# A two-layer hybrid backbone on one core: the order in which the input projections are written, with the first branch's queries behind its keys and the last gate chunk, the last recurrent chunk and the values moved behind the queries

## The chip, the core and the metric

The kernel runs on one core of one Trainium2 chip. The metric is the device time of one execution in microseconds (us); three executions of the kernel before gave 3127.03, 3131.85 and 3134.9 us, and their median, 3131.85 us, is the number to compare with.

The engines are named as the profile names them: PE is TensorE (matmuls), PEld its weight loads, DVE is VectorE, ACT is ScalarE, POOL is GpSimd, and SP is SyncE, whose queue issues every DMA of this kernel. Each engine works through its own instructions in order.

## The reference

The kernel computes two layers of a diffusion backbone on a latent stream of 1024 tokens and a context of 256 tokens, 1024 channels wide. The part of a layer around the change is this:

```
h = modulate(rms_norm(x, g_pre_mix), sh1, sc1);  z = h @ w_in
qa, ka, va, qb, kb, vb, xr, gr = split_columns(z)
qa, ka = apply_axial_rope(rms_norm(qa)), apply_axial_rope(rms_norm(ka))
out_a = global_block_attention(qa, [ka_c, ka], [va_c, va])          # branch a
qb, kb = apply_axial_rope(qb), apply_axial_rope(kb)
out_b = window_sink_attention(qb, kb, vb, kb_c, vb_c, sink)         # branch b
xr = centred_dwconv(xr, conv_w, conv_b)
h_f = directional_rglru(xr, ...)                                    # recurrence, forwards
h_b = directional_rglru(flip(xr), ...)                              # and backwards
out_c = (h_f + flip(h_b)) * gelu(gr)                                # branch c
x = x + gt1 * rms_norm([out_a, out_b, out_c] @ w_out, g_post_mix)
x = x + gt2 * rms_norm(sq_relu_mlp(modulate(rms_norm(x)), w1, w2), g_post_mlp)
```

The first layer also carries the context stream on to its end; the second layer needs it only for keys, values and the recurrence.

## The kernel before

Channels lie on the 128 partitions, tokens along the free axis, in three token tiles: 0 and 1 are the halves of the latent stream (512 tokens each) and 2 is the context (256). Every dense product is made of three matmuls on operands that were split into a high and a low part (`dense`, L497 to L499), over eight blocks of 128 input channels: 24 matmuls for a chunk of 128 output channels and one token tile. The code splits each weight in two: ACT copies it to `whi` (L134) and POOL or DVE makes `wlo` (L475).

**The projections.** The chunks of `w_in` have names: `x0` to `x3` feed the recurrence, `g0` to `g3` its gates (the gelu branch `gr`), `kF` and `kL` are the keys of the first and of the later attention branch, `F0`, `F1` and `L0`, `L1` their queries, and `v` the values of both. In both layers the first branch is b (window attention with a sink) and the later one a. `OPT[l]["ORD"]` writes out the order for layer l: `"g3:201"` is chunk `g3` for the token tiles 2, 0 and 1, `"F0:20"` the first queries for tiles 2 and 0. In layer 1 tile 2 is left out of everything but keys and x. A token `"F;L0:20,L1:20"` weaves two streams: the stacks of branch F (`kstacks`, L836: the keys are read back from DRAM and split into `kh` and `kl`) and the projections after the semicolon. A token `"L"` makes the stacks of the later branch. The results of a query or key chunk go through `qk_evac` (norm for branch a, rotation, DMA to DRAM), those of x through `xr_evac` (the convolution), those of g through `gr_evac`.

**What runs beside them.** Four generators are woven by rates: `conv_all` and `lru_all` for the recurrence, `side`, which walks through `ORD` and then the output projections, and `heads`, which makes the attention. The recurrence goes chunk by chunk, c0 to c3. Chunk c needs `x<c>` and `g<c>`. Its gates are 36 small matmuls (`gate`, L681 to L683), then come ACT's tanh, then exp and ln, and DVE's products and scans (L689, L708, L717, L720, L725); the result `hs` is written to DRAM (L733). tanh and gelu lie in one table set of ACT, exp and ln in another, and the helper `act` loads the other set wherever the order of writing changes from one kind to the other (L130).

`heads` waits until the last value tile exists, and `attend_prep` until all stacks of the branch do. It reads a query tile back (`qf`), splits it on ACT (`qh`), lets PE make scores from the high parts alone (`mx`, L885, L897, L905) and DVE reduce them to row maxima, which PE spreads (`pm`, L918). `attend_units` makes the full scores (`sc`, L954), ACT the exponentials (`prob`), and PE the products with the values (`pv`, L973) and the denominators (`den`, L1004). `out_lru` begins the output projection (`yps`) when all four recurrent chunks are done.

The gates decide one more thing: a recurrent chunk that is begun before the first attention job is prepared makes the gates of both directions at once; one that is begun later makes them one direction after the other, with a longer pause.

A scheduler then places the instructions of each engine in an order near that of writing. The function that names the order of weights from the same table is `entries`.

```
run(chain(*[step(t) for t in cf["ORD"][:cf["NX"]]]))            # the first two tokens of ORD
...
def side():
    for t in cf["ORD"][cf["NX"]:]:
        yield from step(t)
...
def heads():
    yield from wait(lambda: (1, 3) in V)
    yield from attention(jobs, (len(jobs) - 1,))
```

Of the kernel before, what the change touches and what calls it, by code (L numbers as in the profile page):

```python
# [32 lines left out]
    {"SPLIT": ((0,), (2, 1)), "JC": 16, "J": 16, "PRE": 4, "NP": 0, "RB": 1, "OL": (4, 1), "LEAD": 4,  # L33
     "MERGE": 1, "CAHEAD": 2, "NX": 2, "RO": 1.0, "RC": 2.0, "MR": 0.55, "TT0": (0, 2), "ADD_POOL": 4,
     "MUL_POOL": 0,
# [5 lines left out]
     "MUL_POOL": 0,  # L41
# [3 lines left out]
)  # L45
# [1318 lines left out]
```

## Time and profile before

| | |
|---|---|
| median of three executions | 3131.85 us |
| the profiled execution | 3129.46 us |
| its span, first to last instruction | 3127.4 us |
| PE busy | 2922.9 us, 93% |
| PEld, DVE, ACT, POOL busy | 71%, 55%, 40%, 38% |
| mean granted TensorE clock | 0.966 |

The profiled execution is 2.4 us under the median and 2.1 us over its own span. A share of busy time is a mean over stages that have different limits. The granted clock has two levels in this trace, 1.0 (2.4 GHz) and 0.5 (1.2 GHz), so a mean of 0.80 over a stretch says that 40% of it went by at the lower one. The name behind an arrow (`<-`) is what ended the idle time just before an instruction. A wait that is named counts only on the engine that bounds its stage.

### The profile page before, as it was taken

What the parts mean: (1) busy time and instruction counts of PE and PEld (TensorE: products, weight loads), DVE (VectorE), ACT (ScalarE), POOL (GpSimd) and SP (SyncE); (2) the same over time, 40 slices, a digit from 0 to 9 for tenths busy, and PEclk for the clock granted to TensorE, in tenths of its full rate; (3) what the DMA queues carried; (4) which work ended last, traced back from release to release, by engine and by line L of the source; (5) the groups of instructions that cost most, each with busy time, mean ns of one, the idle gap of its engine ahead of it and who ended that gap; (6) DMA issues with size and microseconds to landing.
All of it is one profiled execution on the core that took longest, in us unless ns stands there. A gap on an engine that the chain in (4) does not pass through costs nothing. (4 is left out here: it accounts for less than half of the span.)

```text
span 3127.4 us, 39445 instructions
## 1 busy us (share of the span) xinstructions
PE 2922.9 (93%) x14562; PEld 2227.4 (71%) x14562; DVE 1712.6 (55%) x2714; ACT 1255.1 (40%) x2347; POOL 1189.5 (38%) x919
## 2 busy tenths in 40 slices
PE   6998889998999999999899899689998999999997
PEld 4877544546867888888888688554456888888886
DVE  6765575554476133234884576776454562333465
ACT  4677243355243312213543368733354332122222
POOL 1453343344454222322533333353354553333232
PEclk9999799999999999999999999889998999999999
DMA  7343321123355222111643322330024241111241
GB/s 246 114 149 117 131 85 43 48 66 121 123 174 181 75 65 81 39 39 65 195 134 106 117 65 80 103 110 31 14 86 149 81 139 51 44 44 51 75 145 54
DMA packets 176338, 299.86 MB, mean 96 GB/s; under 512 B 24593, under 2 KB 38417, under 8 KB 176145
## 3 DMA queue, kind: packets, MB, share of 16 engines
q1 hardware_dynamic: 176144, 297.35, 28.9%
q8 instruction: 114, 1.87, 0.2%
q14 instruction: 80, 0.65, 0.1%
HBM read 262.14 MB, written 35.13 MB: 95 GB/s over the span
## 5 line engine op out<-in xcount | busy, mean ns | idle before, releaser
L475 POOL TENSOR_TENSOR wlo<-raw,whi 128x512 fp32r<-128x512 f32 x484 | 687.7, 1437 | 957.7 <-ACT whi L134 319.5
L1191 DVE TENSOR_TENSOR acc<-acc,m 128x512 f32<-128x512 f32 (+1 forms) x488 | 322.3, 676 | 318.7 <-PE m L1184 316.8
L1183 PE MATMUL m<-h1lo,whi 128*128 128x512 f32 (+1 forms) x1296 | 476.6, 369 | 7.3 <-DVE h1lo L1173 7.3
L1184 PE MATMUL m<-h1hi,wlo 128*128 128x512 f32 (+1 forms) x1296 | 474.3, 368 | 0.0
L1182 PE MATMUL m<-h1hi,whi 128*128 128x512 f32 (+1 forms) x1296 | 459.4, 370 | 7.2 <-DVE accc L1191 4.8
L134 ACT ACTIVATE whi<-raw 128x512 fp32r<-128x512 f32 x600 | 352.7, 621 | 149.5 <-DMA raw<-in_w 72.2
L497 PE MATMUL m<-hhi,whi 128*128 128x512 f32 x1024 | 403.3, 395 | 5.3 <-ACT hhi L134 5.3
L498 PE MATMUL m<-hlo,whi 128*128 128x512 f32 x1024 | 399.9, 391 | 2.8 <-DVE hlo L513 2.8
L499 PE MATMUL m<-hhi,wlo 128*128 128x512 f32 x1024 | 399.8, 391 | 0.0
L1173 DVE TENSOR_TENSOR h1lo<-relu,h1hi 128x512 fp32r<-128x512 f32 (+1 forms) x160 | 130.5, 816 | 446.8 <-ACT h1hi L134 446.6
L134 ACT ACTIVATE relu<-m 128x512 f32<-128x512 f32 (+1 forms) x160 | 88.5, 553 | 692.8 <-PE m L499 679.9
L1169 POOL TENSOR_TENSOR relu<-relu 128x512 f32<-128x512 f32 (+1 forms) x160 | 161.8, 1011 | 422.1 <-ACT relu L134 398.9
L1183 PEld LDWEIGHTS m<-h1lo,whi 128*128 128x128 f32 x1296 | 246.8, 191 | 50.2 <-DVE h1lo L1173 9.3
L1182 PEld LDWEIGHTS m<-h1hi,whi 128*128 128x128 f32 x1296 | 244.2, 190 | 53.0 <-DVE accc L1191 6.7
L1184 PEld LDWEIGHTS m<-h1hi,wlo 128*128 128x128 f32 x1296 | 246.6, 190 | 41.0
L497 PEld LDWEIGHTS m<-hhi,whi 128*128 128x128 f32 x1024 | 193.4, 189 | 47.1 <-ACT hhi L134 6.9
L979 POOL TENSOR_TENSOR prob<-prob 128x1024 f32<-128x1024 f32 (+2 forms) x62 | 137.3, 2215 | 229.8 <-ACT prob L134 128.7
L498 PEld LDWEIGHTS m<-hlo,whi 128*128 128x128 f32 x1024 | 193.1, 189 | 44.3 <-DVE hlo L513 3.6
L134 ACT ACTIVATE prob<-sc 128x512 f32<-128x512 f32 (+3 forms) x288 | 141.4, 530 | 206.4 <-PE sc L954 195.7
L499 PEld LDWEIGHTS m<-hhi,wlo 128*128 128x128 f32 x1024 | 192.8, 188 | 41.8 <-issue 1.2
L973 PE MATMUL pv<-prob,vt 128*64 128x512 f32 (+3 forms) x576 | 204.4, 559 | 9.8 <-POOL prob L963 7.0
L497 PE MATMUL zin<-hhi,whi 128*128 128x512 f32 x424 | 172.6, 408 | 0.3 <-ACT gl L134 0.3
(336 smaller groups left out, 5439.3 us busy)
## 6 DMA issues: line engine op xcount, KB each, us to landing
raw<-in_w SPq DMA_DIRECT2D x440, 256.0 KB, 3.5
rawm<-in_w_mod SPq DMA_DIRECT2D x192, 256.0 KB, 3.9
raw<-in_w_in SPq DMA_DIRECT2D x88, 256.0 KB, 3.9
raw<-in_w_out SPq DMA_DIRECT2D x64, 256.0 KB, 3.5
xres<-xs SPq DMA_DIRECT2D x40, 256.0 KB, 5.1
xs<-y SPq DMA_DIRECT2D x32, 256.0 KB, 2.4
fc<-qf SPq DMA_DIRECT2D x30, 256.0 KB, 3.6
tcos<-in_cos SPq DMA_DIRECT2D x24, 256.0 KB, 3.1
```

Of the source, the lines that this page charges most:

```text
L134: r = nc.scalar.activation(out, in_, func, **kw)
L475: (vec if on_dve(key) else gp).tensor_tensor(lo, raw, f(hi), ALU.subtract)
L497: mm(ps, wh, xh, start=(k == first), stop=False)
L498: mm(ps, wh, xl, start=False, stop=False)
L499: mm(ps, wl, xh, start=False, stop=(k == last))
L973: mm(pv[half[h], q0:q1], V[kt, j][:, vcol + 64 * h:vcol + 64 * h + HD], pt[:, h, :], start=(ui == 0), stop=(ui == len(units) - 1), skip_gr ...
L979: eng.tensor_tensor(pacc[0][:, :, q0:q1], pacc[0][:, :, q0:q1], pt, ALU.add)
L1169: gp.tensor_tensor(r, r, r, ALU.mult)
L1182: mm(ps, wh, h1[p][0][:, c0:c1], start=(p == 0), stop=False)
L1183: mm(ps, wh, h1[p][1][:, c0:c1], start=False, stop=False)
L1184: mm(ps, wl, h1[p][0][:, c0:c1], start=False, stop=(p == 1))
L1191: vec.tensor_tensor(a, a, ps, ALU.add)
```

## The change

Both lists `ORD` are written in another order, by the same rule for both layers. Nothing is added and nothing removed: the same tokens stand there, and no other number is touched.

```diff
-     "ORD": ("x0:1", "g0:201", "x1:1", "x2:201", "g1:201", "kF:1", "x3:201", "g2:201", "kL:1", "g3:201", "v", "F0:20", "F1:20", "F;L0:20,L1:20", "F0:1", "L0:1", "F1:1", "L", "L1:1"),
+     "ORD": ("x0:1", "g0:201", "x1:1", "x2:201", "g1:201", "kF:1", "F0:20", "kL:1", "g2:201", "F1:20", "v", "x3:201", "F;L0:20,L1:20", "g3:201", "F0:1", "L0:1", "F1:1", "L", "L1:1"),
...
-     "ORD": ("x0:1", "g0:201", "x1:1", "x2:201", "g1:201", "kF:1", "x3:201", "g2:201", "kL:1", "g3:201", "F0:20", "v", "F1:20", "F;L0:20,L1:20", "F1:1", "F0:1", "L", "L1:1", "L0:1"),
+     "ORD": ("x0:1", "g0:201", "x1:1", "x2:201", "g1:201", "kF:1", "F0:20", "kL:1", "g2:201", "F1:20", "v", "x3:201", "F;L0:20,L1:20", "g3:201", "F1:1", "F0:1", "L", "L1:1", "L0:1"),
```

So `F0:20` and `F1:20` go forwards, `x3` goes behind the values, and `g3` goes behind the stacks of the first branch; the gates and the recurrence of chunk c3, which need `x3` and `g3`, go with them. The four engines carry the same counts of the same instructions in both kernels, but for two more table loads on ACT (22 for 20).

Three places of the instruction order show what follows. The first is SP's queue in layer 0, where the keys of the first branch are read back (`kf<-qkb`). Before, with the recurrent results of chunk c3 (`qf_0_..<-hs`, DRAM tiles 755 to 757) just ahead:

```order
L733 DMA qf_0_2_757<-hsc 128x256
L786 DMA tcos<-in_cos 128x512
L789 DMA tsin<-in_sin 128x512
L353 DMA rawm<-in_w_mod 128x512
L733 DMA qf_0_1_756<-hs 128x512
L842 DMA kf<-qkb_2_733 128x256
L842 DMA kf<-qkb_0_731 128x512
```

And of the change, at the same reads (tiles 752 to 754 are the results of chunk c2):

```order
L733 DMA qf_0_2_754<-hsc 128x256
L353 DMA rawm<-in_w_mod 128x512 x2
L733 DMA qf_0_1_753<-hs 128x512
L733 DMA qf_0_0_752<-hs 128x512
L353 DMA rawm<-in_w_mod 128x512 x2
L468 DMA raw<-in_w_in 128x512 x2
L353 DMA rawm<-in_w_mod 128x512 x3
L842 DMA kf<-qkb_2_733 128x256
```

What stands ahead of the keys is now c2's result, not c3's; c3's results follow 47 rows behind the keys.

The second place is PE in layer 0, at the gate matmuls of chunk c3. Before, the last of them stand between the values (`vps`) and the first queries (`zin`), 150 rows of this list ahead of the first maxima:

```order
L820 MATMUL vps<-whi,hlo 128x256
L681 MATMUL gate<-xh,ghi 128x512
L682 MATMUL gate<-xl,ghi 128x512
L683 MATMUL gate<-xh,glo 128x512
L681 MATMUL gate<-xh,ghi 128x512
L682 MATMUL gate<-xl,ghi 128x512
L683 MATMUL gate<-xh,glo 128x512
L497 MATMUL zin<-hhic,whi 128x256
```

Of the change, where the maxima of the second attention job and the products of the first are in hand:

```order
L683 MATMUL gate<-xh,glo 128x512
L897 MATMUL mx<-khc,qh 128x256
L885 MATMUL mx<-kh,qh 128x384
L973 MATMUL pv<-prob,vt 64x384 x2
L897 MATMUL mx<-khc,qh 128x256
L681 MATMUL gate<-xh,ghi 128x512
L682 MATMUL gate<-xl,ghi 128x512
L683 MATMUL gate<-xh,glo 128x512
```

All 36 gate matmuls of c3 and the 72 projection matmuls of `g3` now stand behind the first maxima of the attention; in layer 1 it is 36 and 48.

The third place is ACT in layer 1, between the first query split (`qh`) and the first exponentials (`prob`). Before:

```order
L134 ACTIVATE kh<-kf 128x512
L134 ACTIVATE lt<-lt,cbuf 128x512 x2
L134 ACTIVATE qh<-qf 128x512
L134 ACTIVATE zsq<-zc 128x512
L134 ACTIVATE rl<-zn,cbuf 128x512
L134 ACTIVATE ry_18267<-rl 128x512
L134 ACTIVATE whi<-raw 128x512 x2
L134 ACTIVATE zc<-zin 128x512
L134 ACTIVATE qm<-pm 65x512
```

Of the change, the last rows ahead of the first exponentials (`gate` and `lt` are c3's tanh):

```order
L134 ACTIVATE lt<-gate_18250,cbuf 128x256
L134 ACTIVATE gate_18265<-gate,cbuf 128x512
L134 ACTIVATE lt<-gate_18265,cbuf 128x512
L134 ACTIVATE whi<-raw 128x512
L134 ACTIVATE gate_18280<-gate,cbuf 128x512
L134 ACTIVATE gate<-gate,cbuf 128x512
L134 ACTIVATE lt<-gate_18280,cbuf 128x512
L130 ACT_TABLE_LOAD
L134 ACTIVATE prob<-sc 128x512 x2
```

c3's tanh and gelu, with a table load on either side, now stand between the first query split and the first exponentials; the keys and the query themselves are no longer mixed with the recurrence's `lt`.

## Rows read from the trace of the kernel before

**Rows 1.** Windows: stretch, length; PE, PEld, DVE, ACT, POOL busy (count); clock; DMA share, GB/s.

```profile
313.80:429.50 115.70, 90.62 (x449) 59.10 (x449) 70.16 (x148) 35.61 (x73) 44.63 (x40) 0.80 0.39 130
429.50:700.00 270.50, 265.77 (x1195) 136.44 (x1195) 163.10 (x264) 112.23 (x228) 111.19 (x79) 1.00 0.16 50
...
2015.50:2094.30 78.80, 65.79 (x283) 40.81 (x283) 57.64 (x114) 27.43 (x54) 39.92 (x34) 0.80 0.32 107
2094.30:2300.00 205.70, 203.57 (x917) 97.72 (x917) 108.33 (x193) 83.58 (x158) 81.12 (x55) 1.00 0.09 31
```

**Rows 2.** Waits of PE from 316 to 429.6: us, times, longest.

```profile
PE zn L779 <- DVE zsq L152: 7.8, 2, 5.5
PE pv L973 <- POOL prob L963: 4.8, 3, 2.2
PE mx L905 <- ACT qhc L134: 3.6, 1, 3.6
```

**Rows 3.** Timeline, layer 0, at the first maxima: start, us, engine [idle before].

```profile
306.05 1.44 POOL L732 TENSOR_TENSOR hs<-hs,gl 128x512 f32<-128x512 f32 x1
...
306.51 1.19 PE L779 MATMUL zn<-zsq,cbuf 128*128 128x256 f32 x2 [2.32 <-DVE zsq L152]
...
307.52 0.33 SPq L733 DMA_DIRECT2D qf<-hs  x1
307.89 1.39 SPq L842 DMA_DIRECT2D kf<-qkb  x3
...
309.66 0.47 ACT L134 ACTIVATE rl<-zn,cbuf 128x256 f32<-128x256 f32 x1 [6.44 <-POOL zc L787]
...
313.76 0.58 PE L885 MATMUL mx<-kh,qh 64*128 64x256 f32 x2 [6.05 <-ACT qh L134]
```

**Rows 4.** Timeline of PE, layer 1, last gate to first maxima.

```profile
1989.87 0.39 PE L683 MATMUL gate<-xh,glo 128*128 128x512 f32 x1
...
1994.81 1.12 PE L779 MATMUL zn<-zsq,cbuf 128*128 128x512 f32 x2 [1.83 <-ACT zsq L134]
2015.46 0.58 PE L885 MATMUL mx<-kh,qh 64*128 64x256 f32 x2 [19.52 <-ACT qh L134]
```

**Rows 5.** Timeline of PE, layer 0: last gate, then 48 projection matmuls, a modulation block.

```profile
275.49 0.39 PE L683 MATMUL gate<-xh,glo 128*128 128x512 f32 x1
275.72 0.28 PE L497 MATMUL zin<-hhic,whi 128*128 128x256 f32 x1
...
278.59 0.40 PE L497 MATMUL zin<-hhi,whi 128*128 128x512 f32 x1
...
284.15 1.07 PE L356 MATMUL pg<-rawm,cbuf 128*32 128x256 f32 x16
...
285.62 0.36 PE L497 MATMUL zin<-hhic,whi 128*128 128x256 f32 x1
```

**Rows 6.** By line, the recurrence's work on DVE: duration ns minimum/median/maximum.

```profile
L689 DVE SCALAR_TENSOR_TENSOR gate<-gate,xc x32: 665/692/693, 125.8 to 1991.1; 128x512 f32<-128x512 f32 x32
L708 DVE SCALAR_TENSOR_TENSOR lt<-a,lt x48: 411/666/1750, 141.1 to 2010.0; 128x512 f32<-128x512 f32 x32, 128x256 f32<-128x256 f32 x16
L717 DVE TENSOR_TENSOR gate<-gate,lt x48: 410/678/1709, 144.7 to 2016.2; 128x512 f32<-128x512 f32 x32, 128x256 f32<-128x256 f32 x16
L725 DVE TENSOR_TENSOR_SCAN a<-gate,a,gate x16: 1254/1514/2279, 155.1 to 2019.4; 128x512 f32<-128x512 f32 x16
```

**Rows 7.** Timeline of ACT, layer 1: the loads on either side of c3's tanh.

```profile
1972.36 1.28 ACT L130 ACT_TABLE_LOAD   x1
1991.85 1.28 ACT L130 ACT_TABLE_LOAD   x1
```

**Rows 8.** Windows at the half clock within the two stretches of the first group.

```profile
337.00:354.20 17.20, 13.09 (x47) 7.47 (x48) 8.46 (x24) 5.06 (x11) 5.36 (x6) 0.50 0.38 122
...
2077.80:2091.50 13.70, 12.77 (x41) 7.14 (x41) 11.84 (x19) 6.80 (x14) 6.11 (x6) 0.50 0.39 135
```

**Rows 9.** Window with a high share of DVE.

```profile
1600.00:1650.00 50.00, 47.56 (x209) 38.75 (x208) 46.58 (x80) 23.68 (x50) 16.00 (x12) 1.00 0.37 121
```

## The prediction, made blind

> **What bounds the kernel now.** I read the page first: PE is busy for 93% of the span (the table above), so only what PE loses can be won. PE loses in two ways, by waiting and by running at the lower clock level after it has waited. I therefore cut the span into windows and looked for those where both happen at once. Apart from the handovers to the MLP they are two, one in each layer, and both at the same place of the program: from the first maxima of the attention (`mx`) to the first output projection (`yps`). In layer 0 that stretch takes 115.7 us, of which PE is busy for 90.6, at a mean clock of 0.80; in layer 1 it takes 78.8 us, 65.8 busy, again at 0.80 [rows 1]. The rest of the attention behind them is full: 265.8 of 270.5 us and 203.6 of 205.7, at clock 1.00 [rows 1]. So behind `yps` nothing is to be had, and ahead of it PE lacks work that could run while the chains of DVE, ACT and POOL go on.
>
> The waits inside say which chains: `zn` waits for DVE's squares (7.8 us), `pv` for POOL's mask (4.8), the second job's `mx` for ACT's split (3.6) [rows 2]. And the timeline shows a stop ahead of the first `mx`. In layer 0 `zn` waits 2.32 us and then `mx` 6.05 us [rows 3]. At that point SP reads the keys back (`kf`, 307.89) only after it has sent chunk c3's result (307.52), which POOL finished at 307.49 [rows 3]: the reader is to see that the keys, long ready, stood behind the last recurrent chunk in SP's queue. In layer 1 the wait is 19.52 us, after 1.83 at `zn` [rows 4]; there the order on ACT shows the key and query splits between c3's `lt` instructions, so they come out at the pace of the recurrence.
>
> **The change, step by step.** It moves work of PE, ACT, DVE and POOL from ahead of the first `mx` to behind it: `g3` and all of c3's gates. What stands at the first `mx` is then c2's recurrence, with the values, `x3` and the later queries between them.
>
> *Moved on PE.* 24 projection matmuls of 256 columns take 278.59 - 275.72 = 2.87 us, 24 of 512 take 284.15 - 278.59 = 5.56, a modulation block 285.62 - 284.15 = 1.47 [rows 5]. `g3` in layer 0 (a context tile and two of 512) is 2.87 + 2 x 5.56 = 14.0 us; the 36 gates are 12 of 256 and 24 of 512 columns, 1.4 + 5.6 = 7.0; with one modulation block 22.5 us. In layer 1 `g3` has two tiles: 11.1 + 7.0 = 18.1 us. In itself this gains nothing: it is taken away ahead of `mx` and added behind it. It gains what it fills of the lost time there.
>
> *The stop ahead of the first `mx`.* From the norm's `rl` on ACT (309.66) to `mx` (313.76) it is 4.1 us of ACT work in a row [rows 3]: two steps of the norm, a copy, three key splits, the query split. ACT has the same row of instructions ahead of `mx` after the change, so that much stays. Of 2.32 + 6.05 = 8.4 us layer 0 keeps 4.1 and saves 4.3; of 1.83 + 19.52 = 21.35 us layer 1 saves 17.2. This holds if c2's recurrence is done by then. From c3's last gate to `mx` it takes 313.76 - 275.49 = 38.3 us in layer 0 [rows 3, 5] and 25.6 us in layer 1 [rows 4]. By the instruction order PE then has, between c2's last gate and the first `mx`, 129 value matmuls of 256 columns (129 x 2.87/24 = 15.4 us), `x3` (14.0), a modulation block (1.5) and `L0:20` (8.4), together 39.3 us; in layer 1 60 value matmuls (7.2), `x3` (14.0) and two tiles of queries (11.1), together 32.3 us. Both are as long as the chain that has to be covered, so I count the saving in full: **21.5 us**. The bounds are 0 and 8.4 + 21.35 = 29.7.
>
> *What the moved work fills.* The room is the idle time of the stretch, 115.7 - 90.6 = 25.1 us and 78.8 - 65.8 = 13.0, and half of the busy time at the half clock, 13.09 / 2 = 6.5 and 12.77 / 2 = 6.4 [rows 1, 8]. So 22.5 us meet 31.6 of room, and 18.1 meet 19.4. Not all fits. The first dozen `mx` and `zn` stand in the same order as before, with the same filler, so the waits there stay. Nor is PE alone: a chunk of the recurrence brings DVE six each of L689, L708, L717 and of scans, 6 x (0.69 + 0.67 + 0.68) + 4 x 1.5 + 2 x 0.7 = 20 us by the medians [rows 6] (the short scans taken at half). In layer 1 DVE was busy for 57.6 of 78.8 us [rows 1]; with 20 more it would fill the old length altogether, and the best that it shows next to a working PE is 46.58 of 50 us [rows 9], 93%. I take 88%, a little under that: the stretch becomes 78 / 0.88 = 88 us, 10 longer, and so about 8 of the 18.1 us are absorbed (0.45). In layer 0 the same sum gives 90 of 115.7 us, so DVE leaves room, and what decides is how much of the idle time lies behind the unchanged beginning: I take 0.6 of 22.5, 13.5 us. Together **21.6 us**; the bounds are 0 (the waits are chains that go on as before) and 40.6.
>
> The Trainium skill (SBUF — State Buffer, section "Who interferes with whom") says that a DVE instruction with two SBUF inputs and a POOL instruction that reads SBUF exclude each other for their whole length. The trace agrees: L708 takes 0.67 us and up to 1.75 [rows 6]. If all of c3's products met POOL's masks, the 20 us of DVE would be some 30 and layer 1 would absorb nothing; that is inside the bounds above.
>
> *Table loads.* Two more on ACT, 1.28 us each [rows 7]: 2.6 us on an engine that is busy for 35.6 of 115.7 and 27.4 of 78.8 us [rows 1]. Hidden, so 0; without that cover 2.6. By the Trainium skill (ScalarE: Activation LUTs, "What ACT_TABLE_LOAD costs") a switch also drains the engine and costs 2.66 us in all, which would make it 5.3.
>
> *The queues.* c3's results now go through SP behind the first keys and queries and 47 rows later; what would wait behind them is the weights of `out_lru`, which needs those results anyway. POOL gets c3's adds and multiplies in stretches where it is busy for 44.6 of 115.7 and 39.9 of 78.8 us [rows 1]: hidden.
>
> *Sum.* 21.5 + 21.6 = 43.1 us. 3129.46 - 43.1 = 3086.4 on the scale of the profiled execution, which lies 2.4 us under the median of the three; so **3089 us** for a median.
>
> **The rivals.**
> *It fills everything.* All 40.6 us are absorbed and the clock stays up, which returns 6.5 + 6.4 us more: 21.5 + 40.6 + 12.9 = 75 us, 3057. For it: room and moved work are nearly equal. Against: DVE in layer 1, and the unchanged beginning.
> *The stop only moves.* c2's chain now has the convolutions of `x3` beside it on ACT and DVE, and if it gets about 20 us longer in both layers, the first `mx` waits as today and the moved work fills nothing: 0 to 8 us, 3124 to 3132. Against: 39.3 against 38.3 and 32.3 against 25.6 us.
> *Slower: the exponentials wait for the tanh.* In the new order c3's tanh and gelu, between two table loads, stand on ACT ahead of `prob`: one group in layer 1, two of half the size in layer 0. Today such a group lasts from one load at 1972.36 to the next at 1991.85, 19.5 us [rows 7], because the gates come at DVE's pace. While it lasts no exponential is made, so no `pv`, and PE has only projections. If PE stood still throughout, 2 x 19.5 = 39 us, and absorbed nothing, it would be 21.5 - 39 = 17.5 us slower, 3149. It decides from the point where the exposed part passes what is saved ahead of `mx` plus what is absorbed. Against: `g3`, the gates themselves and the last query tiles (5.56 us each) stand in PE's order in the same place. The Trainium skill (ScalarE: Activation LUTs, "Table sets: the hidden batching unit") speaks for this rival: calls are to be batched by set, not alternated.
> *It does nothing*, since the scheduler undoes it: the instruction order excludes that at the three places shown.
>
> **Chances.** Part is absorbed, 3065 to 3112: 0.66. Everything, 3050 to 3065: 0.14. The stop moves, 3115 to 3132: 0.09. Slower, about 3149: 0.09. Nothing, 3132: 0.02. From 3058 to 3124 it holds four in five. A change under 0.3% (9.4 us) can't be told from none here; so faster 0.81, same 0.10, slower 0.09.
>
> **What would show it.** Right: the first `mx` comes 25 to 30 us earlier in layer 0 and some 35 in layer 1, with a wait of about 4 us ahead of it; the stretches to `yps` get longer by 5 to 12 us with PE busier and the clock above 0.80; DVE is over 80% busy in layer 1's. Wrong: a wait of over 10 us ahead of `mx`; `sc` or `pv` waiting for ACT over 5 us at a time next to a table load; or new idle time behind `yps`, where the windows are full today.

## The result, and the profile after

The changed kernel takes 3220.52 us (median of four executions, 3216.03 to 3224.63) beside 3132.74 of the kernel before in the same comparison: a ratio of 1.0283 with a 95% interval of 1.0263 to 1.0303, 88 us slower. The prediction was 3089 us, faster, and its range ended at 3124. Of its rivals "the stop only moves" was right about the stop, and the slower one has the right sign but only a small part of the cause.

The profiled execution took 3221.49 us. Its page, first the span, then the engines' busy time:

```profile
span 3219.7 us, 39517 instructions
...
PE 2995.5 (93%) x14562; PEld 2257.1 (70%) x14562; DVE 1690.6 (53%) x2714; ACT 1265.2 (39%) x2349; POOL 1187.4 (37%) x919
```

TensorE executes the same matmuls and is busy for 72.6 us more (2922.9 before), still for 93% of a longer span, at a mean granted clock of 0.957 instead of 0.966. The windows that answer to [rows 1], from the first `mx` to the first `yps` and from there to about the last `pv`, layer 0 and then layer 1 (columns as there):

```profile
297.06:467.20 170.14, 137.21 (x671) 89.80 (x671) 101.28 (x187) 75.41 (x144) 65.60 (x57) 0.81 0.29 96
467.20:738.60 271.40, 269.25 (x1110) 136.39 (x1110) 149.69 (x249) 108.40 (x212) 104.37 (x72) 0.97 0.15 49
2046.53:2168.71 122.18, 99.14 (x420) 63.02 (x420) 81.43 (x142) 58.89 (x111) 51.73 (x41) 0.84 0.24 80
2168.71:2392.10 223.39, 218.54 (x904) 104.96 (x906) 109.00 (x190) 84.64 (x159) 81.37 (x56) 0.97 0.07 22
```

The stretch to `yps` grew from 115.7 to 170.1 us and from 78.8 to 122.2. It is not the same work with a filling: it holds 671 matmuls instead of 449 and 420 instead of 283, of which 124 and 84 are the moved ones (a modulation block of 16 included); the others are attention work that stood behind `yps` before. The idle time in it did not shrink: 33 us instead of 25, and 23 instead of 13. PE's waits from the first `mx` on, in layer 0 (297.06 to 467.2) and in layer 1 (2046 to 2168.71):

```profile
PE den L1004 <- DVE prob L1001: 11.0, 2, 5.7
PE mx L885 <- ACT qh L134: 10.0, 2, 9.4
PE mx L905 <- ACT qh L134: 6.0, 1, 6.0
PE zn L779 <- DVE zsq L152: 6.0, 2, 5.7
...
PE mx L885 <- ACT qh L134: 15.9, 1, 15.9
PE pv L973 <- POOL prob L963: 5.4, 4, 3.2
PE den L1004 <- DVE prob L1001: 3.8, 1, 3.8
```

The longest wait of `mx` at L885, 9.4 and 15.9 us, ends with the first `mx` itself: it is the stop ahead of the stretch, which [rows 3] and [rows 4] show with 6.05 and 19.52, and not a part of the idle time just given. A reader should compare the rest with [rows 2]: the waits named there were for a squaring, a mask and a split; now `den` is added in both layers, and in layer 0 `mx` at L905 waits 6.0 us for the query's split instead of 3.6. They wait for DVE's and ScalarE's work while c3's recurrence runs.

For the whole account I cut every trace at the same instructions of TensorE: each layer's first gate, its first `mx`, the last `pv`, and the first and last MLP tile `m`. All in us; the last column is the median less that of the kernel before in the same comparison.

| kernel | L0 gate to mx | L0 mx to last pv | L0 MLP | L1 gate to mx | L1 mx to MLP | median |
|---|---|---|---|---|---|---|
| before | 195.7 | 392.9 | 1020.7 | 177.8 | 357.7 | |
| after | 177.8 | 444.2 | 1040.6 | 159.2 | 417.1 | +88 |
| layer0_only | 178.0 | 442.2 | 1043.7 | 180.9 | 360.3 | +52 |
| layer1_only | 193.5 | 394.4 | 1017.8 | 161.9 | 404.1 | +30 |
| gates3_early | 193.7 | 388.7 | 1041.4 | 177.0 | 372.7 | +28 |
| gates3_late | 190.3 | 441.4 | 1033.9 | 167.6 | 412.5 | +96 |
| queries_forward | 219.0 | 387.6 | 1022.8 | 173.1 | 356.9 | +14 |
| no_table3 | 177.9 | 437.1 | 1041.1 | 160.8 | 413.1 | +82 |
| light3 | 168.1 | 427.9 | 1016.7 | 163.2 | 398.7 | +25 |
| light3_new | 176.8 | 431.4 | 1040.2 | 159.3 | 410.7 | +70 |
| light3_old | 198.2 | 388.9 | 1024.3 | 179.8 | 356.7 | -4 |
| store_on_pool | 169.2 | 436.8 | 1040.2 | 149.7 | 426.3 | +74 |
| old_store_on_pool | 188.9 | 393.7 | 1025.9 | 174.3 | 356.6 | -13 |

Ahead of `mx` the two layers won 17.9 and 18.6 us, together 36.5, which is less than the 22.5 + 18.1 = 40.6 us of work that the prediction counted out of that place. Behind it they lost 51.3 and 59.4, and layer 0's MLP, which the change doesn't touch, lost 19.9. These are single traces: the MLP took 1017.8 to 1025.9 us in the kernels of the table whose layer 0 keeps `g3` ahead of the values, and over 1040 in all with the new order in layer 0 but *light3*.

What the loss behind `mx` consists of can be read from the same two traces. From the first `mx` to the last `pv` both layers together take 790.6 us instead of 684.2, so 106.4 more. By the prediction's prices 40.6 of that is the moved work. TensorE is idle for 63.0 us there instead of 45.2. And it is busy at the lower clock level for 107.9 us instead of 60.4; a `zin` of 128x512 begins every 0.43 us at that level in the changed kernel and every 0.23 us at the upper one, so by an estimate some 22 us go with the clock. About 26 us remain that none of these explains.

### The profile page after: what moved, and what is told of

Its sections match the earlier page's. It is cut to its first block, busy times and chain, and to the rows that moved or that the text cites. A ratio compares the mean times of both kernels' runs of the same rounds, so it can differ in the third digit from the quotient of the medians.

```text
span 3219.7 us, 39517 instructions
## 1 busy us (share of the span) xinstructions
PE 2995.5 (93%) x14562; PEld 2257.1 (70%) x14562; DVE 1690.6 (53%) x2714; ACT 1265.2 (39%) x2349; POOL 1187.4 (37%) x919
## 5 line engine op out<-in xcount | busy, mean ns | idle before, releaser
L134 ACT ACTIVATE whi<-raw 128x512 fp32r<-128x512 f32 x600 | 357.7, 623 | 547.4 <-PE m L1183 179.1
```

The source lines that it names most:

```text
L134: r = nc.scalar.activation(out, in_, func, **kw)
```

## The experiments

**Each layer alone.** *layer0_only* has the new `ORD` in `OPT[0]` and the old one in `OPT[1]`; *layer1_only* the reverse.

> The new order in layer 0 alone; layer 1 keeps the old one. Theory: each layer's loss is its own. From the changed kernel's trace layer 0 should keep its whole loss, 35.7 us up to the first MLP matmul and some 15 us in the MLP behind it, where the 128x32 modulation matmuls (pg) now stand in small pieces between the others: 3133 + 51 = 3184 us, 3178 to 3190. Rival: the loss in layer 0's MLP is caused by layer 1's order (its weights and modulation are fetched there): then about 3168 here. A second rival, that the losses of the two layers feed each other, would give less than 3160.

> The new order in layer 1 alone. Theory: its own loss, 86 us at the last probability product less the 50 us that layer 1 begins later in the changed kernel, 36 us: 3133 + 36 = 3169, 3163 to 3175, with layer 0 as before to within 1 us. Rival that the MLP's 15 us come from layer 1's order: 3184. Rival that layer 1 only loses because of what layer 0 leaves behind: under 3150.

Measured: 3183.43 (ratio 1.0169, 1.0153 to 1.0186) and 3161.34 (1.0099, 1.0078 to 1.0120), the second 2 us under the range that I had expected. The losses are each layer's own, 52 + 30 of 88, and the MLP's 20 us come with layer 0's order (1043.7 against 1017.8). What I had not expected is in layer 1 of *layer0_only*, whose order is the old one. The window from its first `yps` to its last `pv`, and the same window of the kernel before under it:

```profile
2144.00:2367.00 223.00, 219.21 (x963) 105.46 (x964) 116.37 (x202) 88.98 (x170) 86.94 (x62) 1.00 0.09 29
...
2094.20:2306.00 211.80, 209.43 (x961) 100.95 (x960) 112.67 (x198) 86.49 (x165) 83.63 (x60) 1.00 0.09 30
```

Nearly the same matmuls (one group of four `sc` more) at full clock, PE full in both, and yet 9.8 us more of busy time. Hardly anything is waited for, 3.6 us against 2.3. What differs is the order of the matmuls: the scheduler orders instructions otherwise in places far from the edit. That the order alone makes them dearer is inferred; no run tests it by itself. (The stretch ahead of this `yps` gave back 5.6 us, so layer 1 as a whole is only some 6 us longer there.)

**Which token.** *gates3_early* moves `g3` ahead of the key stacks again in the changed order (first diff); *gates3_late* moves `g3` alone, in the old order, to where the change has it (second); *queries_forward* puts the first branch's queries behind its keys in the old order and keeps `x3`, `g2`, `kL`, `g3` ahead of the values (third). The lines are layer 0's; layer 1 is edited likewise.

```diff
-"x3:201", "F;L0:20,L1:20", "g3:201",
+"x3:201", "g3:201", "F;L0:20,L1:20",
```

```diff
-"g3:201", "v", "F0:20", "F1:20", "F;L0:20,L1:20",
+"v", "F0:20", "F1:20", "F;L0:20,L1:20", "g3:201",
```

```diff
-"kF:1", "x3:201", "g2:201", "kL:1", "g3:201", "v", "F0:20", "F1:20",
+"kF:1", "F0:20", "F1:20", "x3:201", "g2:201", "kL:1", "g3:201", "v",
```

> The changed order with one token moved back: g3 directly behind x3, ahead of the key stacks and the second branch's queries, so that all of c3's gates stand ahead of the first mx again; queries, values and x3 stay where the change put them. Theory (c3's recurrence inside the beginning of the attention is what costs): the losses from the first mx to the first yps go, 30 to 35 us in layer 0 and 30 in layer 1; what stays is the 12 to 15 us of the split modulation matmuls, and up to 15 us are won ahead of the first mx: 3130 to 3155. Rival (the early queries and the values ahead of x3 make c2's chain and the attention late, wherever g3 stands): 3195 to 3220.

> The old order with one token moved: g3 behind the key stacks and the second branch's queries, where the change has it; queries, x3 and values in the old order. Theory (c3's recurrence inside the attention costs): most of the whole loss appears, 3185 to 3225, with waits of den for DVE and of mx for ACT between the first mx and the first yps as in the changed kernel. Rival (the early queries and the late x3 cost): 3130 to 3150, the move of g3 alone being about neutral.

> One part of the change alone: the first branch's queries directly behind its first keys in both layers, and x3, g2, the second keys and g3 behind them in their old order, then the values. c3's gates stay ahead of the first mx, TensorE's order from the first mx on is that of before, and the modulation matmuls stay in 65 pieces. Theory (only c3 inside the attention and the split modulation matmuls cost): 3125 to 3142, the first mx standing behind c3's store as before. Rival (the early queries delay the recurrence's chain, since x3 and g3 come later): 3145 to 3165, with a first mx 10 us later in each layer.

Measured: 3159.60 (1.0091, 1.0076 to 1.0106), 3227.46 (1.0312, 1.0291 to 1.0332) and 3146.36 (1.0043, 1.0029 to 1.0057). The first two lie 5 and 2 us above the ranges of their theories, the third in the range of its rival. `g3` decides: moved alone it costs 96 us, and put back it returns 60 of the 88. With it back, the first stretch of layer 0 takes as long as in [rows 1] again, and the second line shows what runs in it (the lines of DVE in the window):

```profile
316.40:431.60 115.20, 90.21 (x449) 58.87 (x449) 83.65 (x162) 47.91 (x95) 52.86 (x44) 0.80 0.41 131
...
L708 DVE SCALAR_TENSOR_TENSOR lt<-a,lt 128x512 f32<-128x512 f32 (+1 forms) x6 | 4.5, 768 | 0.0
```

c3's gates and tanh stand ahead of `mx` here, but its six products at L708, and behind them those at L717 and all its scans, run inside the stretch: DVE is busy for 83.65 us instead of 70.16, ACT for 47.91 instead of 35.61, and the stretch is no longer for it. So it isn't enough that c3's recurrence runs there. What the stretch doesn't hold is `g3` itself, c3's gates and their tanh and gelu; and the products come at its start (318.6 to 341.7), not in its second half.

The 28 us that stay lie in layer 0's MLP (+20.7) and in layer 1 behind `mx` (+15.0), the places of the order effects above. The early queries cost 14, and the rival's mechanism is there in layer 0, where `x3` and `g3` come later and the first `mx` 23 us later; layer 1 got 5 us shorter.

**What c3 does inside the attention.** *no_table3* replaces c3's tanh and gelu by functions of the same size that need no table (c3's result is left out, as in the other four); *light3* cuts c3's DVE and POOL work to 8 columns, *light3_act* ScalarE's exponentials and logarithms too; *light3_new* and *light3_old* make the cut with the forward scan whole, in the new and the old order. One line of *no_table3* and one of *light3*:

```diff
-act(s, ps, AF.Tanh, scale=0.5, bias=lrubh[:, l, d, gi, c:c + 1])
+act(s, ps, AF.Identity if c == 3 else AF.Tanh, scale=0.0 if c == 3 else 0.5, bias=lrubh[:, l, d, gi, c:c + 1])
...
+w = 8 if c == 3 else TOK[tt]
-vec.scalar_tensor_tensor(t, q, 1.0, t, ALU.add, ALU.mult)
+vec.scalar_tensor_tensor(t[:, 0:w], q[:, 0:w], 1.0, t[:, 0:w], ALU.add, ALU.mult)
```

> The changed kernel, with c3's tanh and gelu replaced by Identity and Copy of the same size, so that c3 needs no table of its own and its ScalarE instructions needn't be grouped between two loads (the gate arithmetic of c3 is left out thereby; counts, sizes and the order of the projections stay). Theory A, the rival on record (the exponentials wait for the tanh group): the loss inside the attention, about 26 us in layer 0 and 30 in layer 1, goes for the most part, 3165 to 3190, and the waits of den for DVE and of mx for ACT there shrink below 2 us each. Theory B (c3's recurrence loads ACT, DVE and POOL at a place where PE hangs on their chains, whatever the tables): 3205 to 3220.

> The changed kernel with c3's DVE and POOL instructions of the recurrence (products, scans, sum and gate product behind the tanh) cut to 8 columns; their number, their order and their waits stay, ScalarE's part stays whole, and c3's result is not computed. It takes some 20 us of DVE and 12 us of POOL out of each layer's attention start. The order of the modulation matmuls in layer 0's MLP comes out in few pieces again (61 in all, 88 in the changed kernel, 65 before), so 12 to 14 us should go there by that alone, to 3207. Theory B1 (DVE's and POOL's load is what delays the attention's chains): 3160 to 3185. Rival B2 (the chain of ScalarE and of TensorE's own order: den, mx and sc stand behind c3's gates and the tanh group): 3197 to 3210.

> As light3, and ScalarE's exponentials and logarithms of c3 (behind the tanh) cut to 8 columns too, so that about 12 us of ScalarE go from each layer's attention start; the tanh, the gelu and the gates' matmuls stay, and TensorE's order is that of light3. Theory B1 (DVE and POOL alone): within 5 us of light3. Theory B3 (ScalarE's load, whose prob stands behind c3's exponentials): 10 to 25 us less than light3. Rival B2: both about 3200.

> As light3, but the forward scan stays whole, which keeps TensorE's order that of the changed kernel in every place, 88 pieces of modulation matmuls included; c3's products, backward scan, sum and gate product are cut to 8 columns (c3's result is left out). Light3 was 63 us under the changed kernel, of which 24 lay in layer 0's MLP, where its order came out otherwise; so 40 us are left for DVE's and POOL's load itself. Theory B1 (the load counts because it stands in the attention's start): 25 to 40 us under the changed kernel, 3180 to 3196. Rival B2 (TensorE's order does it, light3 gained by another order): within 10 us of 3220.

> The same cut in the order of before, whose TensorE order it keeps, 65 pieces included. Theory B1: there c3's load stands ahead of the first mx beside the values and queries, and only shortens the stop there: 5 to 15 us under before, 3117 to 3127. Rival (c3's load costs the same wherever it stands, and so doesn't explain the loss): 25 to 40 us under before, 3092 to 3107.

Measured: 3214.18 (1.0260, 1.0243 to 1.0278), 3157.00 (1.0080, 1.0059 to 1.0100), 3150.55 (1.0052, 1.0032 to 1.0072), 3202.64 (1.0227, 1.0210 to 1.0244) and 3128.48 (0.9989, 0.9978 to 1.0000). The tables are worth 6 us of the 88, which is not clear of the noise (the intervals of *no_table3* and of the changed kernel overlap). *light3_act* lies 6 us under *light3*, again with overlapping intervals, so c3's exponentials and logarithms on ScalarE are worth little there; the theory for them had 10 to 25 us. Light3 looked like the answer and was not: its TensorE order comes out otherwise. With the forward scans whole (*light3_new*), which keeps TensorE's order nearly that of the changed kernel, the cut gives 18 us, less than the 25 to 40 that I had expected; in the old order it gives 4, hardly clear of nothing. So 18 of the 88 are the load of c3's products, backward scans, sums and gate products on DVE and POOL at this place, and of the 46 us between *light3* and *light3_new* 23.5 lie in layer 0's MLP, where c3 has no work, 12.0 in layer 1 behind `mx` and 8.7 ahead of layer 0's first `mx`. The two differ by c3's forward scans and by TensorE's order.

How c3's work gets in the way can be seen in the changed kernel's trace, layer 0. The timeline of ACT, DVE and PE at the first `den`, and of DVE and PE at the next one that waits:

```profile
390.02 1.28 ACT L130 ACT_TABLE_LOAD   x1
...
400.25 1.28 ACT L130 ACT_TABLE_LOAD   x1
401.54 0.72 ACT L134 ACTIVATE ex<-qm,cbuf 65x512 f32<-65x512 f32 x1
...
402.30 0.68 DVE L1001 TENSOR_TENSOR prob<-prob,ex 1x512 f32<-1x512 f32 x1 [3.49 <-ACT ex L134]
...
396.99 0.39 PE L683 MATMUL gate<-xh,glo 128*128 128x512 f32 x1
403.03 1.97 PE L1004 MATMUL den<-prob,cbuf 128*64 128x512 f32 x2 [5.65 <-DVE prob L1001]
...
420.82 3.84 DVE L708 SCALAR_TENSOR_TENSOR lt<-a,lt 128x256 f32<-128x256 f32 x2
424.58 2.02 DVE L1001 TENSOR_TENSOR prob<-prob,ex 1x256 f32<-1x256 f32 x2
426.12 1.12 PE L1004 MATMUL den<-prob,cbuf 128*64 128x256 f32 x2 [5.34 <-DVE prob L1001]
```

PE has finished c3's gates, and the next instruction in its order is `den`. It needs the sink's exponential `ex`, which stands behind c3's tanh group between two table loads. Without tables (*no_table3*) this `den` still waits 2.92 us, since `ex` still stands behind the group. The second `den` waits for DVE, where its product stands behind two of c3's; its wait is 5.33 us without tables and 3.48 with the cut of *light3_new*. Around it lies the window 419 to 443, with three of DVE's dearest groups in it:

```profile
419.00:443.00 24.00, 12.64 (x52) 7.65 (x50) 23.86 (x23) 13.01 (x26) 21.08 (x15) 0.80 0.23 79
...
L708 DVE SCALAR_TENSOR_TENSOR lt<-a,lt 128x512 f32<-128x512 f32 x2 | 4.2, 2123 | 0.0
L717 DVE TENSOR_TENSOR gate<-gate,lt 128x512 f32<-128x512 f32 x1 | 2.3, 2309 | 0.0
L725 DVE TENSOR_TENSOR_SCAN a<-gate,a,gate 128x512 f32<-128x512 f32 x1 | 2.2, 2179 | 0.0
```

DVE is busy for 23.86 of 24 us and PE for 12.64. The products take 2.1 to 2.3 us, where [rows 6] has a median of 0.67, while POOL is busy for 21.08 us. The Trainium skill (SBUF — State Buffer, section "Who interferes with whom") says that only one port pair, shared by DVE and POOL, makes such instructions wait, and that it is an exclusive lock. The trace agrees: DVE's records grow in the stretch in which POOL is full, and in the kernel before the 23 products of 128x512 at L708 that ran without POOL took 0.69 us at most, the three with POOL beside them throughout 1.70 to 1.75.

**The stop ahead of the first `mx`.** *store_on_pool* and *old_store_on_pool* send the recurrent results from POOL's DMA queue, in the new and in the old order.

```diff
-nc.sync.dma_start(out=qd[f"f{4 + c}", tt], in_=hs)
+nc.gpsimd.dma_start(out=qd[f"f{4 + c}", tt], in_=hs)
```

> The changed kernel, the recurrent chunks' results stored from POOL's DMA queue instead of SP's, directly behind the multiply that makes them. Theory: in layer 1 SP sends the keys' loads only at 2040.05, behind the store of c2's result at 2037.04, for which it waited 9.3 us; without that store in the queue the first mx of layer 1 comes 10 to 14 us earlier, and the wait of 15.9 us ahead of it shrinks to under 5; in layer 0 the keys stand behind modulation loads, so nothing changes there. Time 3206 to 3214. Rival: the first mx comes earlier, but the chains behind it take the gain back: 3216 to 3224. Second rival (the keys wait for the query's own chain, not for the store): the first mx stays where it is.

> The kernel before with the same edit: the recurrent results stored from POOL's queue. By the reading in the prediction the keys stood behind c3's store in SP's queue in both layers. Theory: the first mx comes about 4 us earlier in layer 0 and 15 in layer 1, and the time falls by 8 to 20 us, to 3112 to 3125. Rival (the first mx moves, but PE has no other work there and the attention's chains then run no faster, or the splits still come out at the pace of c3 on ACT): within 5 us of 3132.

What they test is shown by the changed kernel's timeline in layer 1 (PE, POOL, SP):

```profile
1997.56 0.40 PE L683 MATMUL gate<-xh,glo 128*128 128x512 f32 x1
...
2035.43 3.25 POOL L732 TENSOR_TENSOR hs<-hs,gl 128x512 f32<-128x512 f32 x2 [1.29 <-DVE hs L731]
...
2037.04 1.99 SPq L733 DMA_DIRECT2D qf<-hs  x2
...
2040.05 1.37 SPq L842 DMA_DIRECT2D kf<-qkb  x3
...
2046.53 0.58 PE L885 MATMUL mx<-kh,qh 64*128 64x256 f32 x2 [15.86 <-ACT qh L134]
```

The keys are still read back behind a store that waits for POOL; it is c2's now. ScalarE, whose key and query splits stand together here, is ready and waits for them, and in *store_on_pool* the stop is a third as long (ACT of the changed kernel, then PE of *store_on_pool*):

```profile
2043.82 0.42 ACT L134 ACTIVATE khc<-kf 128x256 fp32r<-128x256 f32 x1 [9.84 <-DMA kf<-qkb]
...
2019.23 0.58 PE L885 MATMUL mx<-kh,qh 64*128 64x256 f32 x2 [5.37 <-ACT qh L134]
```

Measured: 3206.02 (1.0234, 1.0213 to 1.0255) and 3119.16 (0.9953, 0.9934 to 0.9971). In the changed order PE's idle time between c2's last gate and the first `mx` falls from 12.2 to 4.7 us in layer 0 and from 15.9 to 5.4 in layer 1, about what the prediction had left of it (4.1 each). Layer 1's first `mx` comes 9.5 us earlier, but all of it is lost again behind it (mx to MLP 426.3 instead of 417.1), 9.0 us of it at an `mx` that waits for DVE's maxima; the gain of 14 us comes from layer 0, where I had expected none and the first `mx` came 8.6 us earlier. In the old order the edit makes a kernel that is 13 us faster than before, the fastest here that leaves nothing out. There layer 1's `mx` moved by only 3.5 us, not 15, and the timeline of SP and ACT suggests a reason:

```profile
1995.26 1.33 SPq L842 DMA_DIRECT2D kf<-qkb  x3
...
2008.61 0.71 ACT L134 ACTIVATE lt<-lt,cbuf 128x512 f32<-128x512 f32 x1
2009.22 0.61 ACT L134 ACTIVATE kh<-kf 128x512 fp32r<-128x512 f32 x1
2009.74 1.32 ACT L134 ACTIVATE lt<-lt,cbuf 128x512 f32<-128x512 f32 x2
2010.96 0.61 ACT L134 ACTIVATE qh<-qf 128x512 fp32r<-128x512 f32 x1
```

The loads now go out at 1995.26, but the last split of the keys stands among c3's `lt` on ScalarE. *store_pool_q1* adds the early queries in layer 1, *store_pool_q1_split* also has POOL make those splits there.

```diff
-KHI = ("a", "a")
+KHI = ("a", "p")
...
-act(qh, qf, AF.Copy)
+copy(KHI[l], qh, qf)
```

> The kernel before with the recurrent results stored from POOL's queue, and in layer 1 alone the first branch's queries directly behind its first keys (values and c3 as before, c3 ahead of the attention). The store alone gave 3119; in the run with the queries forward layer 1 was 5.5 us shorter up to its first MLP matmul than before (530.0 against 535.5 from its first gate), of which the store has already given 4.6. Theory (the two gains are partly one): 3113 to 3119. Rival (they add): 3108 to 3113. Second rival (nothing more): 3119 to 3124.

> As the run before, and in layer 1 the keys' and queries' high parts made by POOL instead of ScalarE. With the store on POOL's queue the first mx of layer 1 still stood 19.0 us: the keys' loads were sent at 1995.26, but the split of the last key came at 2009.22 on ScalarE, between c3's lt instructions. Theory: POOL, which has little to do there, makes them as they land, the first mx comes 6 to 10 us earlier, and the time falls by 3 to 8 us against the run before. Rival (PE then waits behind the first mx instead, since the chains of the first job aren't faster, or POOL's masks come late): within 3 us of it.

Measured: 3121.47 (0.9980, 0.9969 to 0.9991) and 3125.61 (0.9988, 0.9978 to 0.9999). Neither adds to the store alone, as the second rival of *store_pool_q1* had it, and the splits on POOL, which I had expected to give 3 to 8 us, give none; with the splits on POOL `mx` waits 14.6 us for POOL's `qh` instead. Whoever makes the splits, they are made late, so in the old order the stop in layer 1 is not a matter of SP's queue alone; what else holds it was not settled.

**Layer 0's MLP.** The modulation matmuls (`pg`, 128x32) of layer 1 are spread over it. *mod_together* holds each block together by order alone, *raw7* gives the raw weights a seventh buffer, and *no_mod_old* and *no_mod_new* leave the blocks out in either order (layer 1's modulation is zero there, and both have five split-weight buffers instead of six). One part of each edit, *raw7*, *no_mod* and *mod_together*:

```diff
-rawp = ctx.enter_context(tc.tile_pool(name="raw", bufs=6))
+rawp = ctx.enter_context(tc.tile_pool(name="raw", bufs=7))
...
-modq1 = list(range(24)) if l == 0 else []
+modq1 = []
...
+tc.add_manual_dep(r.ins, tight["last"].name, nosync, reason="tight")
```

> The changed kernel, with the modulation matmuls of each block in layer 0's MLP held together on TensorE by order alone (no semaphore added). In the changed kernel they stand in pieces of one to four among the 128x128 matmuls, and all 768 passes take 77.9 us where they took 65.3 before. Theory: the pieces cost it: 78 goes back to about 66 and the time falls by 11 to 14 us, 3206 to 3210. Rival (the MLP is longer for another reason, such as weights that come late, and the passes' own longer time is only how the wait shows): less than 4 us.

> The changed kernel with seven buffers instead of six in the pool that holds both the raw weights and the modulation weights. Held together, the modulation matmuls waited 8.2 us for their loads (rawm) in layer 0's MLP, and SP waited 287 us there for POOL's wlo to free a raw buffer, against 145 us before. Theory (in the changed kernel the loads of the modulation weights take their turn in the six buffers at another place, and so come late): a seventh buffer gives back most of layer 0's MLP loss, 3205 to 3212. Rival (the cause is the pieces' order on TensorE, which stays at 85 pieces): 3216 to 3224.

> The order of before, without the modulation blocks of layer 1 that stand in layer 0's MLP (24 blocks, 384 passes of 128x32; layer 1's modulation is left out and set to zero), and with five instead of six buffers for the split weights. From layer 0's first to its last MLP matmul the kernel before took 1020.7 us; the passes' share is some 40 us, so 975 to 985 us here in either theory. It is the base for the next run.

> The changed order with the same two edits (no modulation blocks of layer 1, five split-weight buffers). In the changed kernel layer 0's MLP took 1040.6 us, 20 more than before, and neither holding the modulation matmuls together (1040.9) nor a seventh raw buffer (1044.7) changed that. Theory (the loss comes through the modulation blocks, whose loads and matmuls take turns with the weights): within 5 us of the run without them in the old order. Rival (another part of the MLP's order, such as the splits or the sums, was spoilt): again 15 us or more above it.

Measured: 3218.47 (1.0267, 1.0244 to 1.0290), 3220.92 (1.0277, 1.0258 to 1.0297), 3074.18 (0.9827, 0.9809 to 0.9846) and 3154.56 (1.0084, 1.0066 to 1.0102). The MLP took 1040.9, 1044.7, 974.0 and 982.6 us. So my expectations for *mod_together* and *raw7* failed, and their rivals hold. In *mod_together* the pieces went, but then `pg` waits for its loads, by the wait list of that MLP:

```profile
PE pg L123 <- DMA rawm<-in_w_mod: 10.6, 10, 1.8
```

Without the blocks the two orders differ by 8.6 us instead of 19.9, between what theory (5) and rival (15) had: some 11 seem to come through the blocks and the rest through another part of the order, by one trace each, in a stretch that varied by 8 us between kernels of the old order. In the changed kernel all 768 passes, and a piece in the MLP:

```profile
L356 PE MATMUL pg<-rawm,cbuf 128*32 128x256 f32 x768 | 77.9, 418 | 0.0
...
1154.02 0.62 PE L356 MATMUL pg<-rawm,cbuf 128*32 128x256 f32 x2
1154.57 0.38 PE L1182 MATMUL m<-h1hi,whi 128*128 128x256 f32 x1
```

and in the kernel before:

```profile
L356 PE MATMUL pg<-rawm,cbuf 128*32 128x256 f32 x768 | 65.3, 409 | 0.0
...
1112.25 0.63 PE L356 MATMUL pg<-rawm,cbuf 128*32 128x256 f32 x6
1112.82 0.50 PE L1182 MATMUL m<-h1hi,whi 128*128 128x512 f32 x1
```

A piece of two passes holds TensorE for 0.55 us, one of six for 0.57. The Trainium skill (TensorEngine Tiling (Array Packing), section "Tiling Modes") says that a change of tiling mode drains the engine. The trace agrees in that a piece has a price that hardly depends on its passes: in this MLP of both kernels, pieces that wait for nothing hold TensorE for 0.55 to 0.57 us with two to eight passes, and for 0.98 to 1.00 with ten to sixteen. There are 36 pieces in this MLP in the old order and 57 in the new, and they hold TensorE for 31.3 and 40.5 us. So 9 of the 19.9 us are the pieces' own time, as far as the two traces tell; *mod_together*, with 24 pieces, returns none of it, since the waits for loads take its place.

## Why the prediction was wrong

**The stop ahead of `mx`, 21.5 us saved: wrong, almost nothing was saved.** The step that failed is "Both are as long as the chain that has to be covered, so I count the saving in full". The sum of the work was right, about 40 and 33 us, but from c2's last gate to `mx` it took 53.0 us in layer 0 (244.04 to 297.06) and 49.0 in layer 1 (1997.56 to 2046.53), not 38.3 and 25.6. PE is idle for 28.0 us there, where the waits before were 29.7. The cause is shown: the mechanism named in the prediction, the keys behind a store in SP's queue, was kept with another chunk. With the store on another queue (*store_on_pool*) 10.1 of the 28.0 us are left, though the kernel is only 14 us faster by it and still 74 slower than before. I had read the mechanism correctly and not asked which store would stand there next. The point at which this rival decides I had set at a chain 20 us longer and gave it 0.09; it got 14.7 and 23.4 us longer.

**The moved work, 21.6 of 40.6 us absorbed: wrong, and the largest error.** By that sum the work from `mx` on was to grow by about 19 us in all, and it grew by 110.7. The step that failed is "so about 8 of the 18.1 us are absorbed (0.45)" with its like for layer 0: it treated idle time as room. Nothing was absorbed: TensorE's idle time there grew by 17.8 us and its busy time at the lower clock by 47.5. The idle time was that of chains through ScalarE, DVE and POOL, and `g3` brings work for just those engines into them. Shown of that are 18 us (the cut on DVE and POOL) and, not clear of the noise, 6 (tables). That c3's recurrence runs in the stretch is not by itself the cause, as *gates3_early* shows. The bounds were wrong as well: but for the rival of the tanh they ended at nothing absorbed, and I had excluded that the moved work could make the old work dearer. The room at the lower clock was misread too: [rows 8] has one spell of each stretch, 17.2 and 13.7 us, while a mean clock of 0.80 means 46 and 32; the room was larger than I had counted, and still nothing fell into it.

**The rival "the exponentials wait for the tanh": seen, and small as far as it was tested.** The wait is in the trace (5.65 us at `den`), two groups in layer 0 as it said. The tables are worth 6 us, not 39. The tanh instructions themselves, and the gates ahead of `den` in PE's order, were never taken out of that place by themselves.

**Not in the prediction at all: what the scheduler does elsewhere.** Layer 0's MLP (+19.9) is not touched by the diff, nor is layer 1 in *layer0_only* (+6). I read the order of the program at three places and took the rest as unchanged. With `g3` back in its place 28 us remain of the loss, and they lie in that MLP and in layer 1 behind `mx`.

**Right:** the two table loads (20 to 22 in the program). That they are hidden is not shown. Of the signs of a right prediction only a clock above 0.80 came (0.81 and 0.84): the first `mx` comes 17.9 and 18.6 us earlier instead of 25 to 30 and some 35, and DVE is busy for 67% of layer 1's stretch, not over 80. Of those of a wrong one a wait over 10 us ahead of `mx` came (15.86); the 5.65 us next to a table load are at `den` and not at `sc` or `pv`, and behind `yps` there is no new idle time to speak of (2.2 and 4.9 us).

What stays open: about 60 us go with `g3`'s place, of which 24 were taken apart. The account behind `mx` says in what form the loss comes, 18 us as idle time and some 22 by estimate through the lower clock, but not which of `g3`'s instructions brings it about: the gates and the projections on PE, the tanh group on ACT and the late products on DVE were not moved one by one.

## What to carry to other kernels

Idle time of TensorE is not room by itself: before counting it, ask which engines end the waits, whether the moved work needs them, and what then stands ahead of the instructions that the waits were for. When a chunk is taken out of a queue's way, look what stands there next. And where a scheduler makes the order, compare it over the whole program: an edit in the mixing stage cost 20 us in an MLP that it doesn't touch.

## What the hardware showed unexpectedly

A group of 128x32 matmuls between 128x128 ones holds TensorE for 0.55 us with two passes and for 0.57 with eight, and for 0.98 to 1.00 with ten to sixteen. In *layer0_only* TensorE needed 9.8 us more (219.21 instead of 209.43) for nearly the same matmuls of the attention at full clock with no wait to speak of, 5%; their order differs, and no run tests that by itself. And a store that waits in SP's queue costs by what stands behind it: sent from POOL, it gave 12.7 us of 3132.
